# Expert layer of a two-layer backbone block: the way back from expert slots to token rows once per pair of experts

## The chip, the cores and the metric

One core of a Trainium2 chip runs the whole program. The metric is the device time of one execution in microseconds (us). The engines are TensorE (PE in the profile; PEld is its loading of the stationary operand), VectorE (DVE), ScalarE (ACT), GpSimd (POOL) and SyncE (SP, whose queue issues the weight transfers).

## The reference, cut to what matters

The program computes two layers of a hybrid block over 256 latent tokens and 256 context tokens, model width 1024. The change lies in the second layer's expert network, which works on the 256 latent tokens only:

```python
logits = jnp.dot(xf, router)
top_v, top_i = lax.top_k(logits, 2)
top_w = jax.nn.softmax(top_v, axis=-1)
comb = einsum('tk,tke->te', top_w, one_hot(top_i, 8))
for e in range(8):
    out = out + comb[:, e:e + 1] * swiglu(xf, w_gate[e], w_up[e], w_down[e])
h = h + gt2 * out          # gt2: one gate value per column, the same for all rows
return rms_norm(h, final_norm)
```

`swiglu` is `(silu(x @ w_gate) * (x @ w_up)) @ w_down` with an inner width of 1408. All numbers are float32.

## The kernel before, in words

**Matrix products.** A float32 product is made of three products of a faster type (`fp32r`): each operand is split into a high part and a remainder. For a weight tile, `load` (lines 889 to 896) takes a raw tile `wraw` that a transfer of the SP queue has brought (`fetch`, L886), ScalarE rounds it to `whi` (L893), and VectorE subtracts, `wlo = wraw - whi` (L895). `mm3` (L917 to L919) then issues three matmuls: high by high, high by remainder, remainder by high. In the expert layer there are 7 buffers of `wraw` and 4 each of `whi` and `wlo`; a raw tile is 512 KB (384 KB in the third column chunk).

**Routing.** `moe_route` gives each token a slot in each of its two experts. `moe_pass` with base 0 handles the first 128 slots of every expert; a second pass (base 128) stands in a conditional block and runs only if some expert has more than 128 tokens. Experts are taken in pairs: `gather(g)` (L1603 to L1617) collects the token columns of experts 2g and 2g+1 by matmuls with 0/1 matrices, and `back(...)` (L1619 to L1633) transposes the 0/1 matrices into `oT` (tile `ohT`), one 256-column slice for each expert `ee` of the pair, and makes the slot weights `wsl`. The order of calls is: expert 2g, gather of pair g+1, expert 2g+1.

**One expert** (`expert`, from L1646). Three column chunks of the inner width (512, 512, 384): four weight loads each for gate and up, the results in PSUM banks `mm`, then silu (L1665, ScalarE), product (L1666, VectorE), transposes (L1670) into PSUM banks `aa`, and the split into the inner rows `hFh` and `hFl` (L710, L711). Then 11 loads of the down weight, accumulated over the inner width in the PSUM banks `oo0` and `oo1` (128 slots by 1024 columns).

**The way back.** `scaled` multiplies each half by the slot weight and splits it into `yxh` (ScalarE, L1684) and `yxl` (VectorE, L1685). `finish` then calls `back(nh, i, eng)` four times, for two token tiles `i` and two column halves `nh`. Each call spreads the 128 slots over 128 token rows with two matmuls into one `aa` bank (L1693), multiplies by the gate `g2b` on VectorE into `yt` (L1695), and adds to the token rows `H` (L1696). The add is done by GpSimd; of the last expert's four, three are done by VectorE. `finish` is put on a list and called within the next expert, at its third pair of loads (`AFT = (0, 2)`, L1655); the last expert's is called at once (L1707). So there are eight ways back: seven inside experts 1 to 7, one behind expert 7.

Each tile name has a number of buffers (`s.bufs`, L1718): two for `hFh`, `hFl`, `yxh`, `yxl`, four for `yt`. The PSUM banks of `aa` are 1, 2, 3 and 5, taken in turn. The order of the instructions on each engine is not exactly that of the source: a scheduler of the framework places them by readiness and source order, so that parts of a way back or of a gather can stand between the matmuls of a load.

Of the kernel before, what the change touches and what calls it, by code (L numbers as in the profile page):

```python
# [847 lines left out]
class Full(Kern):  # L848
# [747 lines left out]
    def moe_pass(s, pool, ax, xT_h, xT_l, pos, weights, base):  # L1596
        nc = s.nc
        if base:
            p2 = s.tile(pool, [128, 2, 8], "pos2")
            nc.vector.tensor_scalar(p2, pos, -float(base), None, ALU.add)  # L1600
            pos = p2

        def gather(g):  # L1603

            es = slice(g * 2, g * 2 + 2)
            oh = s.tile(pool, [128, 2, 2, 128], "oh", F32R)
            nc.vector.tensor_tensor(oh, bc(bc(ax["iota"], 2, 1), 2, 1), bc(pos[:, :, es], 128, 3), ALU.is_equal)
            ohf = oh.bitcast(F32)
            xg = [s.tile(pool, [128, 8, 2, 128], t, F32R) for t in ("xgh", "xgl")]
            for k in range(8):  # L1610
                ps = s.tile(s.ps, [128, 512], "aa")
                for j, src in enumerate((xT_h, xT_l)):
                    for i in range(2):
                        nc.tensor.matmul(ps[:, j * 256:j * 256 + 256], src[:, i, k * 128:k * 128 + 128], oh[:, i].rearrange("p a b -> p (a b)"), start=i == 0, stop=i == 1)
                for j in range(2):
                    nc.scalar.copy(xg[j][:, k].rearrange("p a b -> p (a b)"), ps[:, j * 256:j * 256 + 256])
            return es, ohf, xg[0], xg[1]  # L1617

        def back(es, ohf, xgh, xgl):  # L1619
            oT = s.tile(pool, [128, 2, 256], "ohT", F32R)  # L1620
            pt = s.tile(s.ps, [128, 512], "aa")
            for ee in range(2):
                for i in range(2):
                    nc.tensor.transpose(pt[:, (ee * 2 + i) * 128:(ee * 2 + i) * 128 + 128], ohf[:, i, ee], s.cst("ident"))
            nc.scalar.copy(oT.rearrange("p a b -> p (a b)"), pt)
            wsl = s.tile(pool, [128, 2], "wsl")
            pw = s.tile(s.ps, [128, 512], "aa")
            for ee in range(2):
                e = es.start + ee
                for i in range(2):  # L1630
                    nc.tensor.matmul(pw[:, ee:ee + 1], ohf[:, i, ee], s.comb[:, i, e:e + 1], start=i == 0, stop=i == 1)
            nc.vector.tensor_copy(wsl, pw[:, 0:2])
            return xgh, xgl, oT, wsl  # L1633
        G = gather(0)
        if not base:
            s.comb = weights()
        G = back(*G)
        if not base:
            s.moe_rows()
        for g in range(4):  # L1640
            s.expert(pool, g * 2, 0, *G)
            Gn = back(*gather(g + 1)) if g < 3 else None
            s.expert(pool, g * 2 + 1, 1, *G)
            G = Gn

    def expert(s, pool, e, ee, xg_h, xg_l, oT, wsl):  # L1646
        nc = s.nc
        hF_h = s.tile(pool, [128, 11, 128], "hFh", F32R)
        hF_l = s.tile(pool, [128, 11, 128], "hFl", F32R)
        for c in range(3):  # L1650
            cw = 512 if c < 2 else 384
            pg = s.tile(s.ps, [128, 512], "mm")
            pu = s.tile(s.ps, [128, 512], "mm")
            for kh in range(4):
                if (c, kh) == AFT and s.pending:  # L1655
                    s.pending.pop()()
                for nm, ps in (("g", pg), ("u", pu)):
                    hi, lo = s.load(f"x{nm}{e}{c}{kh}")
                    hi = hi.rearrange("p (k m) -> p k m", k=2)
                    lo = lo.rearrange("p (k m) -> p k m", k=2)  # L1660
                    for kk in range(2):
                        k = kh * 2 + kk
                        s.mm3(ps[:, :cw], xg_h[:, k, ee], xg_l[:, k, ee], hi[:, kk], lo[:, kk], k == 0, k == 7)
            sl = s.tile(pool, [128, 512], "xs")
            nc.scalar.activation(sl[:, :cw], pg[:, :cw], AF.Silu)  # L1665
            nc.vector.tensor_mul(sl[:, :cw], sl[:, :cw], pu[:, :cw])  # L1666
            pt = s.tile(s.ps, [128, 512], "aa")
            n = cw // 128
            for q in range(n):
                nc.tensor.transpose(pt[:, q * 128:q * 128 + 128], sl[:, q * 128:q * 128 + 128], s.cst("ident"))  # L1670
            s.split(hF_h[:, c * 4:c * 4 + n].rearrange("p a b -> p (a b)"), hF_l[:, c * 4:c * 4 + n].rearrange("p a b -> p (a b)"), pt[:, :cw])
        py = [s.tile(s.ps, [128, 512], t) for t in ("oo0", "oo1")]
        for f in range(11):
            hi, lo = s.load(f"xd{e}{f}")
            for nh in range(2):
                ns = slice(nh * 512, nh * 512 + 512)
                s.mm3(py[nh], hF_h[:, f], hF_l[:, f], hi[:, ns], lo[:, ns], f == 0, f == 10)
        wc = wsl[:, ee:ee + 1]
        parts = []

        def scaled(nh):
            yh = s.tile(pool, [128, 512], "yxh", F32R)
            yl = s.tile(pool, [128, 512], "yxl", F32R)
            nc.scalar.activation(yh, py[nh], AF.Copy, scale=wc)  # L1684
            nc.vector.scalar_tensor_tensor(yl, py[nh], wc, yh.bitcast(F32), ALU.mult, ALU.subtract)  # L1685
            parts.append((yh, yl))

        def back(nh, i, eng):
            ns = slice(nh * 512, nh * 512 + 512)
            ps = s.tile(s.ps, [128, 512], "aa")  # L1690
            o = oT[:, ee, i * 128:i * 128 + 128]
            for j in range(2):
                nc.tensor.matmul(ps, o, parts[nh][j], start=j == 0, stop=j == 1)  # L1693
            t = s.tile(pool, [128, 512], "yt")
            nc.vector.tensor_mul(t, ps, s.g2b[:, ns])  # L1695
            eng.tensor_tensor(s.h[2 + i][:, ns], s.h[2 + i][:, ns], t, ALU.add)  # L1696
        scaled(0)
        scaled(1)

        def finish():  # L1700
            for i in range(2):
                for nh in range(2):
                    back(nh, i, nc.vector if e == 7 and (nh or i) else nc.gpsimd)

        s.pending.append(finish)
        if e == 7:
            s.pending.pop()()  # L1707

# [6 lines left out]

    def moe(s, pool, out):
        nc = s.nc
        s.bufs.update(xs=2, hFh=2, hFl=2, yxh=2, yxl=2, xgh=2, xgl=2, ohT=2, oh=2, wsl=2, yt=4)  # L1718
        r = s.moe_route(pool)
        s.moe_pass(pool, *r, 0)  # L1720
        s.moe_overflow(pool, r)
# [5 lines left out]
        for i in range(2):  # L1727
            for nh in range(2):
                o = s.h[2 + i][:, hs[nh]]
                (nc.vector if i and nh else nc.gpsimd).tensor_tensor(o, o, s.fn[:, hs[nh]], ALU.mult)  # L1730
        for i in range(2):
            j = 4 + 2 * i
            rs, f = s.rsqrt1(pool, s.ss[:, j:j + 1], 1e-6 * D, f"fr{i}", s.ss[:, j + 1:j + 2])
            nc.vector.tensor_scalar(rs, rs, f, None, ALU.mult)  # L1734
            for nh in range(2):
                o = s.h[2 + i][:, hs[nh]]
# [207 lines left out]
```

## Time and profile before

| | |
|---|---|
| median of 3 runs | 2430.71 us (2422.58 to 2433.34) |
| profiled execution, its own time | 2412.98 us |
| its span, first to last instruction | 2411.2 us |
| mean granted TensorE clock | 0.970 |
| stretch of the experts with ways back inside | about 2016 to 2390 us of the span |

In the profile L12 is line 12 of the kernel; `out<-in` are tile names; a number after "idle before" or in brackets is the time that an engine stood idle in front of an instruction, and `<-` names the instruction that ended the wait. Matmuls overlap, and their ends are modelled, so that the pace of TensorE is read from the starts of its instructions. "DVE x3" in a timeline means three merged instructions.

### The profile page before, as it was taken

The numbers are of one execution on the slowest core, as the hardware profiler recorded it, in microseconds if no ns is written. First come the engines' busy times: TensorE is split into PE (matmuls) and PEld (weight loads), VectorE is DVE, ScalarE is ACT, GpSimd is POOL, SyncE is SP. The second block draws the span as 40 slices with busy tenths as digits, with TensorE's granted clock in tenths as the row PEclk, the third lists the DMA queues.
The fourth block names the chain that finished last, engine by engine and source line by source line (L and its number), as shares of the span: only waits on it lengthen the run. The fifth ranks groups of instructions, "written<-read, shape, count | busy, mean of one in ns | idle before, by whom it ended". The sixth has DMA issues, their size and how long they took to land. (4 is left out here: it accounts for less than half of the span.)

```text
span 2411.2 us, 41643 instructions
## 1 busy us (share of the span) xinstructions
PE 2262.6 (94%) x15772; PEld 1785.6 (74%) x15772; DVE 1538.5 (64%) x2994; ACT 1170.4 (49%) x2150; POOL 355.6 (15%) x307
## 2 busy tenths in 40 slices
PE   7989999999999989999998999999998989999996
PEld 4767777787667767778876777878867768878775
DVE  5776666655566453333227678777567578888897
ACT  4544444544543342222226554565363457777765
POOL 1311112101002210000013221130111211111120
PEclk9999999999999999999999999999899989999998
DMA  7343432223235424443223333322325658988895
GB/s 259 110 141 127 139 122 71 76 87 117 94 113 157 160 81 162 169 162 104 95 79 124 111 113 117 115 65 91 114 71 162 216 174 320 336 306 318 309 319 192
DMA packets 160609, 373.69 MB, mean 155 GB/s; under 512 B 18016, under 2 KB 35424, under 8 KB 160400
## 3 DMA queue, kind: packets, MB, share of 16 engines
q1 hardware_dynamic: 160400, 370.94, 45.9%
q8 instruction: 126, 2.06, 0.4%
q14 instruction: 83, 0.68, 0.1%
HBM read 345.18 MB, written 25.69 MB: 154 GB/s over the span
## 5 line engine op out<-in xcount | busy, mean ns | idle before, releaser
L895 DVE TENSOR_TENSOR wlo<-wraw,whi 128x512 fp32r<-128x512 f32 (+4 forms) x666 | 652.6, 1001 | 347.9 <-ACT whi L893 334.7
L893 ACT CAST whi<-wraw 128x512 fp32r<-128x512 f32 (+4 forms) x666 | 536.8, 820 | 557.2 <-PE mm L918 226.6
L917 PE MATMUL fl<-xh,whi 128*128 128x512 f32 (+1 forms) x816 | 317.0, 389 | 2.8 <-ACT whi L893 2.7
L919 PE MATMUL fl<-xh,wlo 128*128 128x512 f32 (+1 forms) x816 | 306.7, 376 | 6.7 <-DVE wlo L895 6.5
L918 PE MATMUL fl<-xl,whi 128*128 128x512 f32 (+1 forms) x816 | 302.4, 371 | 0.0
L919 PEld LDWEIGHTS fl<-xh,wlo 128*128 128x128 f32 x816 | 157.7, 193 | 31.6 <-DVE wlo L895 10.0
L917 PEld LDWEIGHTS fl<-xh,whi 128*128 128x128 f32 x816 | 158.0, 194 | 27.9 <-issue 6.0
L918 PEld LDWEIGHTS fl<-xl,whi 128*128 128x128 f32 x816 | 158.2, 194 | 21.3 <-issue 4.7
L917 PE MATMUL mm<-xh,whi 128*128 128x512 f32 (+1 forms) x416 | 165.6, 400 | 2.0 <-ACT pad L1797 1.0
L919 PE MATMUL mm<-xh,wlo 128*128 128x512 f32 (+1 forms) x416 | 162.5, 391 | 3.2 <-DVE wlo L895 3.1
L918 PE MATMUL mm<-xl,whi 128*128 128x512 f32 (+1 forms) x416 | 163.5, 393 | 0.0
L918 PE MATMUL mm<-wlo,xgh 128*128 128x512 f32 (+1 forms) x384 | 146.5, 381 | 15.3 <-DVE wlo L895 14.8
L917 PE MATMUL mm<-whi,xgh 128*128 128x512 f32 (+1 forms) x384 | 144.3, 378 | 0.2 <-ACT xs L1665 0.2
L919 PE MATMUL mm<-whi,xgl 128*128 128x512 f32 (+1 forms) x384 | 143.7, 374 | 0.0
L1696 POOL TENSOR_TENSOR H<-H,yt 128x512 f32<-128x512 f32 x29 | 56.1, 1960 | 392.5 <-DVE yt L1695 392.5
L918 PEld LDWEIGHTS mm<-wlo,xgh 128*128 128x128 f32 x384 | 72.2, 188 | 37.0 <-DVE wlo L895 27.0
L917 PEld LDWEIGHTS mm<-xh,whi 128*128 128x128 f32 x416 | 78.3, 189 | 27.3 <-ACT whi L893 4.9
L919 PEld LDWEIGHTS mm<-xh,wlo 128*128 128x128 f32 x416 | 78.4, 188 | 20.9 <-DVE wlo L895 4.9
L636 PEld LDWEIGHTS ch<-Pb,TT 128*128 128x128 f32 x512 | 71.8, 194 | 26.2 <-DVE Pb L630 17.3
L918 PEld LDWEIGHTS mm<-xl,whi 128*128 128x128 f32 x416 | 78.6, 189 | 16.3 <-DVE xl L711 0.8
L646 DVE SCALAR_TENSOR_TENSOR Sd<-ch,e2c,Se 64x64 f32<-64x64 f32 x192 | 53.8, 280 | 56.0 <-PE ch L641 53.4
L636 PE MATMUL ch<-Pb,TT 128*128 128x64 f32 x512 | 79.3, 278 | 8.9 <-DVE Pb L630 8.1
(527 smaller groups left out, 4688.1 us busy)
## 6 DMA issues: line engine op xcount, KB each, us to landing
wraw<-in_ws_dram SPq DMA_DIRECT2D x284, 512.0 KB
wraw<-in_ws_dram SPq DMA_DIRECT2D x302, 256.0 KB
wraw<-in_w_mod_dram SPq DMA_DIRECT2D x96, 256.0 KB
wraw<-in_ws_dram SPq DMA_DIRECT2D x64, 384.0 KB
wraw<-in_w_mod_dram SPq DMA_DIRECT2D x32, 512.0 KB
wm<-in_w_mod_dram SPq DMA_DIRECT2D x32, 256.0 KB
spg<-stg SPq DMA_DIRECT2D x24, 256.0 KB
mth<-spg SPq DMA_DIRECT2D x24, 256.0 KB
```

The lines of the kernel that those rows point to most:

```text
L636: mm(ch[:, 128 + h * 64:192 + h * 64], U.TF[:, (2 * c + h) * 64:(2 * c + h) * 64 + 128], Pb[:, hs[h]], start=True, stop=True)
L646: nc.vector.scalar_tensor_tensor(S[hr, k, hr], ch[hr, o], e2c[hr, c, :], Se[hr, hr], ALU.mult, ALU.add)
L893: s.nc.scalar.copy(hi, raw)
L895: s.follow(s.nc.vector.tensor_sub(lo, raw, hi.bitcast(F32)))
L917: mm(out, ah, bh, start=start, stop=False)
L918: mm(out, ah, bl, start=False, stop=False)
L919: mm(out, al, bh, start=False, stop=stop)
L1696: eng.tensor_tensor(s.h[2 + i][:, ns], s.h[2 + i][:, ns], t, ALU.add)
```

## The change

The two experts of a pair now share one way back. An even expert leaves its scaled parts (`yxh`, `yxl` of both halves) on `s.pair`; the odd one adds its own and puts one `finish` on the list, which is called at the same place in the following expert (or at once behind expert 7). Each call of `back` accumulates four matmuls in one `aa` bank, two for each expert, and is followed by one gate product and one add. The scaled tiles get four buffers instead of two, the inner rows one instead of two.

```diff
@@ moe_pass
+        s.pair = []
         G = gather(0)
@@ expert
         def back(nh, i, eng):
             ns = slice(nh * 512, nh * 512 + 512)
             ps = s.tile(s.ps, [128, 512], "aa")
-            o = oT[:, ee, i * 128:i * 128 + 128]
-            for j in range(2):
-                nc.tensor.matmul(ps, o, parts[nh][j], start=j == 0, stop=j == 1)
+            for q, parts in enumerate(pair):
+                for j in range(2):
+                    nc.tensor.matmul(ps, oT[:, q, i * 128:i * 128 + 128], parts[nh][j], start=q == j == 0, stop=q == j == 1)
             t = s.tile(pool, [128, 512], "yt")
             nc.vector.tensor_mul(t, ps, s.g2b[:, ns])
             eng.tensor_tensor(s.h[2 + i][:, ns], s.h[2 + i][:, ns], t, ALU.add)
         scaled(0)
         scaled(1)
+        s.pair.append(parts)
...
-        s.pending.append(finish)
+        if ee:
+            pair, s.pair = s.pair, []
+            s.pending.append(finish)
         if e == 7:
             s.pending.pop()()
@@ moe
-        s.bufs.update(xs=2, hFh=2, hFl=2, yxh=2, yxl=2, xgh=2, xgl=2, ohT=2, oh=2, wsl=2, yt=4)
+        s.bufs.update(xs=2, hFh=1, hFl=1, yxh=4, yxl=4, xgh=2, xgl=2, ohT=2, oh=2, wsl=2, yt=4)
```

## Rows read from the trace of the kernel before

**Rows 1.** Busy time by engine, 2016 to 2389.5 us: PE, PEld, DVE, ACT, POOL; clock, DMA share, GB/s
```profile
2016.00:2389.50 373.50, 357.06 (x1668) 291.61 (x1666) 331.84 (x323) 267.09 (x327) 54.84 (x28) 1.00 0.88 310
```
**Rows 2.** Waits of 2015 to 2390 us: who for whom, total us, times, longest
```profile
POOL H L1696 <- DVE yt L1695: 350.5, 10, 72.2
...
PEld mm L918 <- DVE wlo L895: 27.0, 28, 1.6
...
PE mm L918 <- DVE wlo L895: 14.8, 24, 1.1
...
ACT whi L893 <- DMA wraw<-in_ws_dram: 4.9, 17, 0.8
```
**Rows 3.** Timeline of VectorE in and after the first way back
```profile
2016.69 2.49 DVE L1695 TENSOR_TENSOR yt<-aa,SU 128x512 f32<-128x512 f32 x4 [0.90 <-PE aa L1693]
2019.09 7.60 DVE L895 TENSOR_TENSOR wlo<-wraw,whi 128x1024 fp32r<-128x1024 f32 x4
2026.61 0.67 DVE L1666 TENSOR_TENSOR xs<-xs,mm 128x512 f32<-128x512 f32 x1
```
**Rows 4.** Timeline of GpSimd: the first way back's adds
```profile
2017.46 7.01 POOL L1696 TENSOR_TENSOR H<-H,yt 128x512 f32<-128x512 f32 x4 [72.24 <-DVE yt L1695]
```
**Rows 5.** Weight remainders (L895) in 2010 to 2030 us, then in 1960 to 2010 us: ns min/median/max
```profile
L895 DVE TENSOR_TENSOR wlo<-wraw,whi x9: 1212/1225/2305, 2012.1 to 2028.3; 128x1024 fp32r<-128x1024 f32 x9
...
L895 DVE TENSOR_TENSOR wlo<-wraw,whi x34: 950/1224/1227, 1960.5 to 2005.7; 128x1024 fp32r<-128x1024 f32 x26, 128x768 fp32r<-128x768 f32 x8
```
**Rows 6.** All instructions of L1695, L1696 and L1693: count, ns min/median/max
```profile
L1695 DVE TENSOR_TENSOR yt<-aa,SU x32: 674/682/692, 2016.7 to 2394.8; 128x512 f32<-128x512 f32 x32
...
L1696 POOL TENSOR_TENSOR H<-H,yt x29: 1267/2265/2278, 2017.5 to 2392.5; 128x512 f32<-128x512 f32 x29
...
L1693 PE MATMUL aa<-yxh,ohT x32: 388/395/503, 2016.0 to 2391.0; 128*128 128x512 f32 x32
```
**Rows 7.** Timeline of weight loading (PEld): the three late remainders after the first way back
```profile
2021.15 0.19 PEld L918 LDWEIGHTS mm<-wlo,xgh 128*128 128x128 f32 x1 [0.54 <-DVE wlo L895]
...
2023.38 0.19 PEld L918 LDWEIGHTS mm<-wlo,xgh 128*128 128x128 f32 x1 [1.01 <-DVE wlo L895]
...
2025.61 0.19 PEld L918 LDWEIGHTS mm<-wlo,xgh 128*128 128x128 f32 x1 [1.01 <-DVE wlo L895]
```
**Rows 8.** Timeline of PE: undisturbed pace, then first and last matmul of that way back
```profile
2014.42 0.39 PE L919 MATMUL mm<-whi,xgl 128*128 128x512 f32 x1
...
2015.79 0.39 PE L919 MATMUL mm<-whi,xgl 128*128 128x512 f32 x1
2016.02 0.40 PE L1693 MATMUL aa<-yxh,ohT 128*128 128x512 f32 x1
...
2017.65 0.40 PE L1693 MATMUL aa<-yxl,ohT 128*128 128x512 f32 x1
2017.89 0.39 PE L917 MATMUL mm<-whi,xgh 128*128 128x512 f32 x1
```
**Rows 9.** Weight-load waits at 2010:2030, 2115:2137, 2334:2356 (experts 1, 3, 7), us, times, longest
```profile
PEld mm L918 <- DVE wlo L895: 2.6, 3, 1.0
...
PEld mm L918 <- DVE wlo L895: 5.4, 5, 1.6
...
PEld mm L918 <- DVE wlo L895: 3.9, 4, 1.2
```
**Rows 10.** The same waits at 2060:2080 and 2170:2192 (experts 2 and 4)
```profile
PEld mm L918 <- DVE wlo L895: 2.7, 3, 1.2
...
PEld mm L918 <- DVE wlo L895: 3.2, 4, 1.2
```
**Rows 11.** Timeline of the end: TensorE, then VectorE behind expert 7, then ScalarE
```profile
2389.38 0.39 PE L919 MATMUL oo<-whi,hFl 128*128 128x512 f32 x1
2390.08 1.32 PE L1693 MATMUL aa<-yxh,ohT 128*128 128x512 f32 x4 [0.31 <-ACT yxh L1684]
...
2391.74 1.89 DVE L1695 TENSOR_TENSOR yt<-aa,SU 128x512 f32<-128x512 f32 x3 [0.27 <-PE aa L1693]
...
2395.56 1.03 DVE L1696 TENSOR_TENSOR H<-H,yt 128x512 f32<-128x512 f32 x1
2399.87 0.63 ACT L1079 ACTIVATE njunk<-H 128x512 f32<-128x512 f32 x1 [5.28 <-DVEq L1751]
```
**Rows 12.** Last reads of the inner rows by expert 0, first write by expert 1
```profile
L919 PE MATMUL oo<-whi,hFl x16: 392/392/392, 1995.1 to 2005.6; 128*128 128x512 f32 x16
...
L710 ACT CAST hFh<-aa x1: 587/587/587, 2028.0 to 2028.0; 128x512 fp32r<-128x512 f32 x1
```
**Rows 13.** As Rows 1, between ways back: two of eight such stretches
```profile
1985.00:2005.00 20.00, 20.00 (x97) 17.11 (x96) 18.89 (x19) 16.85 (x19) 0.00 (x0) 1.00 0.98 376
...
2080.00:2115.00 35.00, 35.00 (x177) 30.26 (x177) 28.68 (x30) 27.18 (x39) 0.00 (x0) 1.00 0.93 334
```

## The prediction

> **What bounds the kernel now.** I read four views, in this order. First the busy time of the expert stage [rows 1]: of 373.5 us TensorE is busy for 357, VectorE for 332, and the transfers hold their engines for 0.88 of the time; the clock is at its upper level, 2.4 GHz, throughout. So TensorE sets the pace and two others stand close behind. Second the waits [rows 2]: the only large wait of TensorE is for the weight remainders `wlo` that VectorE makes. It is 27.0 us by the weight loads and 14.8 us by the matmuls, whose modelled ends hide a part. GpSimd's 350 us of waiting costs nothing; it has little to do. Third the timelines, to find where those waits lie. The seven ways back inside the stage behave alike: four gate products on VectorE, 2.49 us together, then four remainders in 7.60 us [rows 3], that is up to 2.3 us each, where one takes 1.22 us with GpSimd idle [rows 5]. Just then GpSimd adds four tiles to the token rows [rows 4]; an add, too, takes 2.27 us in the middle and 1.27 us alone [rows 6]. So VectorE loses time twice, by the products and by the adds beside its remainders. Fourth the pace of TensorE. Undisturbed, six matmuls, one weight tile, take 2015.79 - 2014.42 = 1.37 us [rows 8]. After a way back the first matmul with a remainder comes every 2.23 us, each time after 1.01 us of waiting [rows 7]. One such wait thus costs 2.23 - 1.37 = 0.86 us, 0.85 of what the row shows.
>
> In the seven windows that hold the ways back of experts 1 to 7 the row says 2.6, 2.7, 5.4, 3.2, 5.4, 3.9 and 3.9 us [rows 9, 10]; experts 5 and 6 repeat the rows of experts 3 and 7. The sum is 27.1, the whole of [rows 2]. Between ways back TensorE does not stop: 20.0 of 20 and 35.0 of 35 us [rows 13].
>
> **The change part by part.** *Matmuls.* Their number stays: eight ways back with eight become four with sixteen. A matmul of the way back takes (2017.89 - 2016.02) / 8 = 0.23 us [rows 8], like any other. TensorE gains nothing by itself.
>
> *Four ways back fall away*, those called inside experts 1, 3, 5 and 7; those inside 2, 4 and 6 and the one behind expert 7 remain. VectorE is spared 16 products of 0.68 us, 10.9 us [rows 6]. GpSimd is spared 16 adds, and with each group of four VectorE is spared three slow remainders (2.31 instead of 1.22 us [rows 5]; the mean of 7.60 / 4 in [rows 3] says the same): 12 x 1.09 = 13.1 us. Together 24.0 us of VectorE, 6.0 for each way back. What TensorE gets of that is its own wait: 2.6 + 5.4 + 5.4 + 3.9 = 17.3 us, times 0.85, 14.7 us. The bounds are 17.3 us (the rows as they stand) and 9.5 us (the share 17.3 / 27.1 of the 14.8 us in [rows 2]). I take 14.7, which comes from starts. That it is less than 24.0 fits: part of each delay is swallowed by remainders made ahead.
>
> Why both slow down is a matter of the subtraction, which reads two tiles, meeting an add which reads two. The Trainium skill, SBUF — State Buffer, section Who interferes with whom, says that a VectorE instruction with two SBUF inputs contends with a GpSimd one that reads SBUF, and that the later of the two stands still until the other is done. By that rule, with this trace's 1.27 us add, a remainder would be held for 1.27 us and the 13.1 above would be 12 x 1.27 = 15.2; the trace, with 1.09, comes near to it and decides.
>
> *Three ways back grow* to sixteen matmuls. Their waits today are 2.7 + 3.2 + 3.9 = 9.8 us by the row (experts 2 and 4, and expert 6, whose row is that of expert 7) [rows 9, 10], 8.3 at 0.85. The added 8 x 0.23 = 1.87 us of TensorE work is moved, not new, and needs no weight tile, so VectorE can catch up under it. At best it covers 1.87 each, 5.6 us together. At worst the three are like the two costly ones of today (5.4 x 0.85 = 4.6 each), 5.5 us more. The nearest row is [rows 3, 8], where the eight matmuls stand in one block: the fourth product ends at 2019.18, 1.29 us after the block (2017.89). With four matmuls to a product (0.93 us) VectorE keeps step, and its last product ends about 0.68 us after the block. I take that difference, 0.6 us each, a gain of 1.8 us.
>
> *The end.* Behind expert 7 there are eight more matmuls, 1.87 us at most. TensorE stands for 0.47 us between 2389.38 and 2390.08 (0.70 less one matmul) until ScalarE has `yxh`, and the first expert's two matmuls fit there. From then on VectorE sets the pace, from 2391.74 to 2396.59 with four products and three adds [rows 11]; TensorE needs 0.93 us per tile against 0.68 + 0.7. After it ScalarE only goes on at 2399.87. Cost 0 to 1.87 us; I take 0.5, since only the second tile can come late. The one GpSimd add and three VectorE adds there stay as they are. If the cover failed, all eight matmuls would lie open.
>
> *Buffers.* Four scaled tiles are needed, since the even expert's wait through the odd one; they are freed by the way back early in the next even expert, long before its own `scaled`. The SP queue issues weight transfers when a raw tile is free, that is after its remainder; a VectorE that is less late frees them earlier, and no transfer is moved. One buffer of inner rows means that the first split of an expert must wait for the last down matmul before it. The last read is at 2005.6, the next write at 2028.0 [rows 12]: 22 us apart, cost nothing. What covers it is that the whole of the first column chunk lies between.
>
> *Sum.* 14.7 + 1.8 - 0.5 = 16.0 us. The profiled execution took 2412.98 us by its own time (span 2411.2 and 1.8 around it), so it would take 2397.0. It lies 17.7 us under the median of the three runs; I take the same 16.0 off that median: 2430.7 - 16.0 = 2414.7 us. Half a per cent, 12.2 us, is about what a measurement of this kernel can tell from no change; the forecast lies beyond it.
>
> **The rivals.** *The transfers take over.* Between ways back they hold their engines for 0.93 to 0.98 of the time at 334 to 376 GB/s [rows 13]; over the stage it is 0.88 and 310. Faster experts want 310 x 373.5 / 357.5 = 324 GB/s on the mean, which fits, but the pauses in which the raw tiles fill up today are the very stalls that go. ScalarE already waits 4.9 us for raw tiles [rows 2], without TensorE noticing. For it speaks the 0.98; against it that TensorE is never stopped in those stretches. Should half of the gain turn into waits for `wraw`, the time is 2422.7 us, within half a per cent.
>
> *The bunched way back starves TensorE.* Place: the three that remain. If VectorE's four products stand in its queue ahead of the remainders, the remainders and, behind them, TensorE's next weight tiles wait for sixteen matmuls instead of eight. Price: each costs double the worst of today, 9.2 us, 27.6 together against 23.0 for all seven now (27.1 x 0.85), 4.6 more, and the end's whole 1.87: 2430.7 + 6.5 = 2437.2 us, slower. It decides once TensorE stops for over 7 us in one way back. Against it speaks that the longest single wait is 1.6 us [rows 2] and that the bunch spares TensorE weights while it lasts.
>
> *One buffer binds.* If an expert's split, or the transposes in front of it, waited for the expert before, TensorE would idle for up to the eleven down tiles, 11 x 1.37 = 15.1 us, at seven borders: 2536 us. It takes a scheduler that puts the next expert's first chunk before the last down matmuls; the 22 us of [rows 12] exclude it nearly wholly. The Trainium skill, Trainium Kernel Development and Optimization, section Best Practices, advises two buffers so that transfers and compute overlap; no transfer writes these tiles.
>
> *It doesn't do what it says.* If the adds on GpSimd were no cause of the slow remainders, only the products would count: 10.9 of 24.0, a gain of 7.3 us, 2423.4 us.
>
> **How the numbers follow.** Forecast 0.70 (of it 0.63 beyond half a per cent), transfers 0.14 (0.03 beyond), bunched 0.09 (half of it beyond 12.2 us slower), one buffer 0.01, adds no cause 0.06 (0.02 beyond). So faster 0.68, same 0.26, slower 0.06. The forecast's own range: gain at most 14.7 + 5.6 = 20.3, at least 9.5 - 1.87 = 7.6 with the three unchanged, so 2410.4 to 2423.1. Runs lay 8.1 below and 2.6 above the median; with 5 us below and 6 above it becomes 2405 to 2429, which takes in the transfers and the adds and leaves out the other two.
>
> **What would show it.** Right: four groups of GpSimd adds, behind expert 7 included; L1695 16 times; L1693 still 64 matmuls; 9 slow remainders instead of 21; the wait of weight loads for `wlo` near 8 us in total; expert 7 and its like without a stop. Wrong: a wait for `wraw` in front of TensorE's, a `wlo` wait of over 15 us in three places, an `hFh` split that waits for `oo` matmuls, or a stage of the same length with fewer waits.

## The result, and the profile after

| | before | after |
|---|---|---|
| median of the runs | 2420.88 us (20 runs, 2410.45 to 2433.34) | 2407.51 us (20 runs, 2400.22 to 2430.70) |
| ratio, 95% interval | | 0.9945, 0.9929 to 0.9962 |
| span of the profiled execution | 2411.2 us | 2404.7 us |
| last router matmul to end of span | 472.2 us | 459.1 us |

The change makes the kernel 0.55% faster: 2420.88 × 0.0055 = 13.3 us. The spans differ by only 6.5 us, and the first thing to learn from this case is why. The router's matmuls (L1526) stand at the end of the part in front of the experts, which the change does not touch. One row each, before and then after, of all instructions of L1526 (count, ns, first and last start):

```profile
L1526 PE MATMUL aa<-aR,hT x32: 180/256/382, 1928.0 to 1939.0; 128*128 128x8 f32 x32
```
```profile
L1526 PE MATMUL aa<-aR,hT x32: 184/256/382, 1934.8 to 1945.7; 128*128 128x8 f32 x32
```

In the execution that was profiled after, the same instructions ended 6.7 us later. Counted from there, the expert layer takes 2411.2 - 1939.0 = 472.2 us before and 2404.7 - 1945.7 = 459.1 us after: 13.2 us less before rounding, which agrees with the 13.3 of the runs. All stretches below are counted so, and are called "the stretch". The expectations of eight experiments count from a later mark, the last `xTl` subtraction on GpSimd; their figures (465.4 us before, 452.2 after) are some 7 us smaller than those here.

Waits after, 2010 to 2384 us (who for whom, total us, times, longest), answering to [rows 2]:

```profile
POOL H L1697 <- DVE yt L1696: 316.9, 3, 119.1
...
PEld mm L918 <- DVE wlo L895: 9.3, 12, 1.2
...
PE mm L918 <- DVE wlo L895: 4.7, 9, 0.8
PEld aa L1671 <- DVE xs L1667: 4.5, 9, 0.7
ACT whi L893 <- DMA wraw<-in_ws_dram: 4.1, 12, 0.8
...
PEld mm L917 <- ACT whi L893: 1.9, 3, 0.8
PEld aa L1694 <- ACT yxh L1685: 1.8, 4, 0.5
```

TensorE's wait for remainders fell from 27.0 to 9.3 us, and ScalarE's for raw tiles from 4.9 to 4.1. Busy time by engine in the same window, answering to [rows 1] (PE, PEld, DVE, ACT, POOL; clock, DMA share, GB/s):

```profile
2010.00:2384.00 374.00, 366.56 (x1744) 304.10 (x1742) 319.09 (x318) 277.51 (x352) 25.01 (x12) 1.00 0.89 320
```

TensorE is now busy for 366.6 of 374 us; the transfers went from 310 to 320 GB/s. GpSimd's timeline after shows the four places of its adds, the last a single add behind expert 7 (VectorE does the other three there):

```profile
2071.01 9.03 POOL L1697 TENSOR_TENSOR H<-H,yt 128x512 f32<-128x512 f32 x4 [119.06 <-DVE yt L1696]
2178.53 7.99 POOL L1697 TENSOR_TENSOR H<-H,yt 128x512 f32<-128x512 f32 x4 [98.49 <-DVE yt L1696]
2285.86 7.99 POOL L1697 TENSOR_TENSOR H<-H,yt 128x512 f32<-128x512 f32 x4 [99.34 <-DVE yt L1696]
2386.46 1.27 POOL L1697 TENSOR_TENSOR H<-H,yt 128x512 f32<-128x512 f32 x1 [92.62 <-DVE yt L1696]
```

**Stops by expert.** For every matmul I took the distance to the next one's start and subtracted the usual distance of that kind (0.23 us for 512 columns [rows 8]); what is left, summed from the first `yxh` of one expert to that of the next, is called the stops of that expert. It counts every cause, not only `wlo`.

| us | e1 | e2 | e3 | e4 | e5 | e6 | e7 | odd | even |
|---|---|---|---|---|---|---|---|---|---|
| before | 2.5 | 2.8 | 4.9 | 3.3 | 4.9 | 4.3 | 4.3 | 16.6 | 10.4 |
| after | 0.3 | 2.3 | 0.8 | 3.3 | 1.2 | 4.3 | 1.9 | 4.1 | 9.9 |

The gain is 12.5 us in the odd experts, whose way back has gone, and only 0.5 in the even ones, whose way back has grown. Behind the first `yxh` of expert 7 the rest took 21.9 us before and 21.4 after. 13.0 and 0.4 (before rounding) make 13.4; the stretches say 13.2.

**Why the even experts stayed as they were.** Timeline of TensorE after, the matmuls of the way back inside odd experts (three of its rows):

```profile
2124.22 0.40 PE L1694 MATMUL aa<-yxh,ohT 128*128 128x512 f32 x1
2124.45 0.40 PE L1694 MATMUL aa<-yxl,ohT 128*128 128x512 f32 x1
...
2333.34 0.50 PE L1694 MATMUL aa<-yxh,ohT 128*128 128x512 f32 x1
```

Expert 2's half of the pair is issued inside expert 3, from 2124 to 2161 us, once its scaled tiles are ready (the first at 2120); so are those of experts 4 and 6, inside 5 and 7. When `finish` comes in expert 4, only eight matmuls remain, at 2172.86 to 2179.89; before they stood at 2172.81 to 2179.85. Only in expert 2 are sixteen issued in one place (2063.71 to 2073.78, with other matmuls between them), and only there did the stops shrink, by 0.5 us. VectorE's timeline of expert 4 after, around its products:

```profile
2177.76 1.88 DVE L1696 TENSOR_TENSOR yt<-aa,SU 128x512 f32<-128x512 f32 x3
2179.56 1.35 DVE L895 TENSOR_TENSOR wlo<-wraw,whi 128x1024 fp32r<-128x1024 f32 x1
2180.84 0.68 DVE L1696 TENSOR_TENSOR yt<-aa,SU 128x512 f32<-128x512 f32 x1
2181.44 8.44 DVE L895 TENSOR_TENSOR wlo<-wraw,whi 128x1024 fp32r<-128x1024 f32 x5
```

Products and remainders mix, and five remainders in a row take 8.44 us beside GpSimd's adds: the pattern of [rows 3], unchanged in the ways back that are left. Over the stage 8 remainders take more than 1.5 us, called slow below, where 21 did before.

### The profile page after: what moved, and what is told of

Read it like the earlier page. It is cut to its first block, busy times and chain, and to the rows that moved or that the text cites. A ratio compares the mean times of both kernels' runs of the same rounds, so it can differ in the third digit from the quotient of the medians.

```text
span 2404.7 us, 41593 instructions
## 1 busy us (share of the span) xinstructions
PE 2262.7 (94%) x15772; PEld 1788.6 (74%) x15772; DVE 1514.2 (63%) x2978; ACT 1168.2 (49%) x2150; POOL 327.3 (14%) x291
## 5 line engine op out<-in xcount | busy, mean ns | idle before, releaser
L895 DVE TENSOR_TENSOR wlo<-wraw,whi 128x512 fp32r<-128x512 f32 (+4 forms) x666 | 637.1, 977 | 362.6 <-ACT whi L893 350.7
L636 PEld LDWEIGHTS ch<-Pb,TT 128*128 128x128 f32 x512 | 71.5, 193 | 26.5 <-DVE Pb L630 17.7
L1697 POOL TENSOR_TENSOR H<-H,yt 128x512 f32<-128x512 f32 x13 | 26.3, 2049 | 409.5 <-DVE yt L1696 409.5
```

The source lines that it names most:

```text
L636: mm(ch[:, 128 + h * 64:192 + h * 64], U.TF[:, (2 * c + h) * 64:(2 * c + h) * 64 + 128], Pb[:, hs[h]], start=True, stop=True)
L895: s.follow(s.nc.vector.tensor_sub(lo, raw, hi.bitcast(F32)))
```

## The experiments

Each kernel was run once or as often as is given, beside the kernel before on the same chip. Since the part in front varied by 28 us over these executions (last router matmul at 1938.0 to 1966.1), the stretch is compared. It was 459.1 and 458.7 us in two executions of the changed kernel, and 472.2 in the kernel before and again in one with the same order of instructions (one_inner_buffer); from these two pairs of executions, a thin base, I take a difference of 1 us or more for real. The part of the stretch in front of expert 0's first `yxh`, where no way back stands, took 66.3 to 67.0 us, but 65.7 in three_experts and 67.7 in lead_of_three; these two need a closer look.

| | stretch | wait for `wlo` | slow remainders | stops odd / even |
|---|---|---|---|---|
| before | 472.2 | 27.0 | 21 | 16.6 / 10.4 |
| after | 459.1 | 9.3 | 8 | 4.1 / 9.9 |
| products_only | 460.7 | 14.5 | 9 | 5.6 / 10.6 |
| adds_only | 462.7 | 15.6 | 15 | 7.8 / 10.3 |
| one_inner_buffer | 472.2 | 27.0 | 21 | 16.6 / 10.3 |
| two_places | 460.5 | 11.9 | 11 | 3.8 / 11.2 |
| spread_chunk3 | 461.4 | 9.5 | 12 | 5.3 / 11.4 |
| spread_late | 465.9 | 6.5 | 12 | 5.9 / 15.2 |
| lead_of_three | 462.4 | 13.3 | 9 | 5.6 / 11.9 |
| adds_on_vector | 459.2 | 4.7 | 0 | 3.3 / 11.0 |
| three_experts | 456.9 | 5.0 | 6 | 5.4 / 7.9 |
| sum_kept_apart | 454.5 | 2.0 | 0 | 4.3 / 2.9 |
| sum_apart_early | 454.6 | 3.6 | 0 | 5.3 / 3.0 |

The wait is the row "PEld mm <- DVE wlo" over the whole span; the down loads have a row of their own (`oo`), which is 0 to 1.0 us except in spread_late.

### Which half of a way back costs: the products or the adds

products_only is the kernel before without the adds of experts 0, 2, 4 and 6:

```diff
-            eng.tensor_tensor(s.h[2 + i][:, ns], s.h[2 + i][:, ns], t, ALU.add)
+            if e % 2:
+                eng.tensor_tensor(s.h[2 + i][:, ns], s.h[2 + i][:, ns], t, ALU.add)
```

> The kernel before, with the adds of the ways back of experts 0, 2, 4 and 6 left out (these experts do not reach the output); their matmuls and gate products stay, so that in experts 1, 3, 5 and 7 VectorE still does four products but has GpSimd idle beside it. Read: the row of weight loads waiting for wlo over the stage (27.0 us before, of it 17.3 in the four odd experts; 9.3 after the change) and the stretch from the last xTl subtraction on GpSimd to the end of the span (465.4 us before, 452.2 after). Theory (VectorE falls behind by products plus slowed remainders, and a lead of about 3 us that it has swallows the first part): the products alone are 2.7 us per way back and are nearly swallowed, so the row falls to 10 to 12 us. Rival A (every us of VectorE counts alike): 45 per cent of the odd experts' wait stays, 16 to 19 us. Rival B (the products alone matter): it stays at 24 to 27 us.

adds_only is the kernel before without the products of those experts; the adds take a scaled tile instead:

```diff
-            t = s.tile(pool, [128, 512], "yt")
-            nc.vector.tensor_mul(t, ps, s.g2b[:, ns])
+            if e % 2:
+                t = s.tile(pool, [128, 512], "yt")
+                nc.vector.tensor_mul(t, ps, s.g2b[:, ns])
+            else:
+                t = parts[nh][0].bitcast(F32)
```

> The kernel before, with the gate products of experts 0, 2, 4 and 6 left out: GpSimd adds the scaled tile itself (yxh) to the token rows, so that these experts reach the output without their gate, way back and remainder; the matmuls stay. In experts 1, 3, 5 and 7 the adds still run beside the remainders, without products. Theory (sum of both against a lead): the slowed remainders alone are 3.3 us per way back, a little over the lead of 3, so the row of weight loads waiting for wlo falls to 10 to 14 us; the adds can start earlier than before and still slow three remainders per group to 2.3 us, 21 in all. Rival A (every us alike): 18 to 20 us. Rival B (the products alone matter): 9 to 10 us, with 21 slow remainders. Rival C (the adds alone matter): 24 to 27 us.

Measured: 2410.81 and 2430.57 us, the kernel before 2420.78; adds_only came to its experts 27 us late, and its stretch is 9.5 us shorter than before. Waits for remainders, products_only and then adds_only:

```profile
PEld mm L918 <- DVE wlo L895: 14.5, 17, 1.2
```
```profile
PEld mm L918 <- DVE wlo L895: 15.6, 20, 1.2
```

What follows: leaving out the adds alone brings 11.5 of the change's 13.2 us (472.2 to 460.7), with two buffers of the scaled tiles as before, so that the four buffers of the change can be worth 1.6 us at most. Leaving out the products alone brings 9.5, though some of the adds' effect goes with them, as below. Together that is more than the change: the two causes overlap. With the products alone the odd experts stop for 5.6 us, with the adds alone for 7.8, with neither for 4.1 (the changed kernel), with both for 16.6. So the products alone cost 1.5 us; the 3.7 us of the adds (7.8 - 4.1) are no full price. The rows came out above what I had expected of either kernel, and adds_only had 15 slow remainders, not 21: its adds do not wait for products and start earlier, and in experts 1, 3, 5 and 7 they slowed 0, 1, 2 and 3 remainders, where three had been slow in each. In expert 7, the only one with three, TensorE's weight loads waited 3.6 us for `wlo` with the adds alone and 3.9 before. So the adds can stop TensorE by themselves, once they meet remainders.

An estimate from the prediction's 6.0 us of VectorE for each way back (24.0 / 4) and the 12.5 us that four of them cost, 3.1 each, would be that about 3 us per expert are free. Products alone, at 2.7 us, agree with it. Expert 7 of adds_only does not: its three slow remainders are 3.2 us longer than undisturbed ones, and expert 7 still took 52.9 us from one first `yxh` to the next, 50.7 in the changed kernel and 53.2 before. A fixed free share is not shown.

### Is the single buffer of inner rows free

The kernel before with the new buffer counts of `hFh` and `hFl` alone:

```diff
-        s.bufs.update(xs=2, hFh=2, hFl=2, yxh=2, ...
+        s.bufs.update(xs=2, hFh=1, hFl=1, yxh=2, ...
```

> The kernel before with one buffer of the inner rows hFh and hFl in place of two, nothing else changed; the order of the instructions on every engine is that of the kernel before. If the single buffer costs nothing (22 us lie between the last read and the next write), the stretch from the last router matmul to the end is 472.2 us within 0.5. If the split of an expert's first chunk has to wait, it is longer by the wait, and ScalarE's cast L710 shows a wait for the oo matmuls instead of the transposes.

Measured: 2426.65 us, the kernel before 2424.19 (17 runs, 2411.15 to 2436.16). The weight loads of remainders in this kernel (busy us, mean ns, then idle us before them and what ended it):

```profile
L918 PEld LDWEIGHTS mm<-wlo,xgh 128*128 128x128 f32 x384 | 72.3, 188 | 36.9 <-DVE wlo L895 27.0
```

What follows: the wait is 27.0 us and the stretch 472.2 us, as before. The single buffer costs nothing, so the change's difference lies in the ways back.

### Would the remaining work hurt less if it were spread

My theory after the first runs was that a way back comes as one burst against a lead of four weight tiles, so that the same work spread over an expert would fit. two_places calls half of `finish` at the third and half at the seventh pair of loads:

```diff
-AFT = (0, 2)
+AFT = ((0, 2), (1, 2))
...
-                if (c, kh) == AFT and s.pending:
-                    s.pending.pop()()
+                for _ in range(2 if (c, kh) in AFT and s.pending else 0):
+                    s.pending.pop(0)()
...
```

> The changed kernel, with the shared way back called in two halves, two of its four tiles at the third pair of loads of the first column chunk and two at the third pair of the second chunk. The work is the same. Theory (a delay of VectorE stops TensorE only as far as it exceeds a lead of about 3 us, and the lead comes back between the halves, eight loads at 1.37 against 1.13 us): each half delays by 3 us, the row of weight loads waiting for wlo falls from 9.3 to 0 to 4 us and the stretch from the last xTl subtraction to the end from 452.2 to about 446 us. Rival (the total of VectorE's work in an expert counts, wherever it stands): 8 to 10 us and 451 to 453 us.

spread_chunk3 moves the whole of it into the third chunk (`AFT = (2, 2)`):

> The changed kernel, with the shared way back called whole, but at the third pair of loads of the third column chunk (one place later by two chunks); by the framework's order its four products then stand 5, 9 and 8 instructions apart on VectorE. Theory of the burst: like the run called tile by tile, row 0 to 4 us and 443 to 447 us. Rival (the place in the source decides, a whole way back stays a burst): 8 to 10 us and 451 to 453 us.

spread_late makes the four calls of `back` one at a time, among the down loads:

```diff
-                if (c, kh) == AFT and s.pending:
-                    s.pending.pop()()
...
+            if f in (1, 3, 5, 7) and s.pending:
+                s.pending.pop(0)()
             hi, lo = s.load(f"xd{e}{f}")
...
```

> The changed kernel, with the shared way back called tile by tile at the down loads 1, 3, 5 and 7 of the following even expert, in place of all at once at the third pair of loads. The framework may issue a tile's matmuls and product earlier; in the order of VectorE's instructions the four products of a way back now stand four and more weight tiles apart. Theory (TensorE stops because products and slowed remainders come in one burst at a place where VectorE's lead is small; the two halves in the run before stood only 4 to 15 us apart, in and beside the same column chunk): each single tile delays by 0.68 + 1.1 us, which is within the lead; the row of weight loads waiting for wlo falls from 9.3 to 0 to 4 us, and the stretch from the last xTl subtraction to the end from 452.2 to 443 to 447 us. Rival (VectorE's total work in an expert counts, wherever it stands): 8 to 12 us and 451 to 454 us, as with the two halves.

lead_of_three has three buffers of `whi` and `wlo` instead of four:

> The changed kernel with three buffers of whi and wlo in place of four in the expert layer, so that VectorE and ScalarE can be one weight tile (1.37 us) less ahead of TensorE. Theory (the lead swallows the first part of each delay): each of the three shared ways back inside the stage stops TensorE some 1.4 us longer, the row of weight loads waiting for wlo rises from 9.3 to 13 to 17 us, and the stretch to the end from 452.2 to 456 to 461 us. Rival (VectorE has no lead from the buffers at these places, since it is behind already): 9 to 11 us and 452 to 454 us.

Measured: 2413.14 us for two_places (before 2420.78); 2410.03, 2423.35 and 2417.38 us for the others (before 2424.63). Their stretches are 1.4, 2.3, 6.8 and 3.3 us longer than the changed kernel's. Waits of spread_late, 2010 to 2395 us:

```profile
PEld oo L918 <- DVE wlo L895: 7.2, 10, 1.2
PEld mm L918 <- DVE wlo L895: 6.5, 11, 1.0
PEld mm L917 <- ACT whi L893: 5.9, 8, 0.8
```

and its VectorE timeline around one tile:

```profile
2098.68 0.69 DVE L1696 TENSOR_TENSOR yt<-aa,SU 128x512 f32<-128x512 f32 x1 [1.68 <-PE aa L1694]
2099.29 4.05 DVE L895 TENSOR_TENSOR wlo<-wraw,whi 128x1024 fp32r<-128x1024 f32 x3
```

What follows: spreading gained nothing anywhere, and my theory of a burst at one place falls in that form. Added to the 452.2 us from which the expectations count, their differences give 453.6, 454.5 and 459.0 us, above the rival's figures too. Two things speak in the rows. First, each single add slows a whole remainder (12 for 12 adds in spread_late), while four adds in a row slow fewer than three (8 for 12). Second, a product that is called late waits in VectorE's queue for TensorE's matmuls, 1.68 us here with remainders behind it; over the stage such waits add up to 11.3 us in spread_late, 5.7 in spread_chunk3 and 0.8 in two_places, which is the order of their stretches. The lead does count: one buffer less cost 3.3 us, a little under the least that I had expected. But not as the theory had it: 0.8 us of it lies in front of expert 0's first `yxh` and 1.4 in expert 1, which hold no way back; the three experts with ways back took 1.2 us more together, not 1.4 each. How VectorE would do with ways back spread wide and without such queue waits stays open.

### Taking the slow remainders away

adds_on_vector lets VectorE do the adds of the three ways back inside:

```diff
-                    back(nh, i, nc.vector if e == 7 and (nh or i) else nc.gpsimd)
+                    back(nh, i, nc.vector if e < 7 or nh or i else nc.gpsimd)
```

> The changed kernel, with the adds of the three shared ways back inside the stage done by VectorE in place of GpSimd. Theory (an add on GpSimd costs VectorE three slowed remainders per four adds, 3.3 us): no remainder of the three ways back is slow any more, but VectorE does 4 x 0.7 = 2.8 us of adds, so the row of weight loads waiting for wlo stays at 7 to 10 us and the stretch to the end at 451 to 453 us. Rival (an add in VectorE's own queue delays it fully, one on GpSimd is mostly free): 16 us or more and over 457 us. Rival (the standstill beside GpSimd costs more than the row shows): under 4 us and under 448 us.

Measured: 2408.98 us (before 2420.78). No remainder is slow and the wait for remainders is halved to 4.7 us, yet the stretch is the changed kernel's. VectorE's timeline in expert 6:

```profile
2287.10 1.28 DVE L1696 TENSOR_TENSOR yt<-aa,SU 128x512 f32<-128x512 f32 x2
2288.30 1.28 DVE L1697 TENSOR_TENSOR H<-H,yt 128x512 f32<-128x512 f32 x2
2289.50 1.28 DVE L1696 TENSOR_TENSOR yt<-aa,SU 128x512 f32<-128x512 f32 x2
2290.70 1.28 DVE L1697 TENSOR_TENSOR H<-H,yt 128x512 f32<-128x512 f32 x2
2291.90 4.62 DVE L895 TENSOR_TENSOR wlo<-wraw,whi 128x1024 fp32r<-128x1024 f32 x4
```

and the busy time of TensorE there (first column after the length: PE; the clock is the third from the end):

```profile
2290.00:2294.00 4.00, 0.89 (x5) 0.69 (x5) 4.00 (x6) 0.23 (x1) 0.00 (x0) 1.00 0.28 113
2294.00:2298.00 4.00, 4.00 (x12) 3.09 (x11) 3.66 (x4) 2.03 (x2) 0.00 (x0) 0.57 0.91 297
2298.00:2302.00 4.00, 4.00 (x21) 3.09 (x20) 3.05 (x4) 2.92 (x5) 0.00 (x0) 1.00 0.95 366
```

What follows: the stretch is within what was expected, the wait for remainders below it. Four products and four adds stand in one block of 4.8 us ahead of the remainders, and TensorE stops once for 3.5 us. Afterwards it runs slower: its matmuls start every 0.43 us instead of 0.23 (12 in these 4 us, 21 in the next, by the rows), and the granted clock is 0.57 on the mean, so part of the time at the lower level, 1.2 GHz. The row of waits counts the 3.5 us but not what follows them. The stops of experts 4 and 6 (4.4 and 5.5 us, before 3.3 and 4.3) hold both.

### Fewer ways back still

three_experts makes one way back for three experts (0 to 2, 3 to 5, 6 and 7), with six scaled tiles, three `ohT` and one `xs` and one `oh`:

```diff
...
-        if ee:
+        if e % 3 == 2 or e == 7:
...
```

> The changed kernel with a way back once per three experts (behind experts 2 and 5, called in 3 and 6, and the last two at the end): six scaled tiles, three tiles ohT, and one buffer each of oh and xs to make room. Two ways back lie inside the stage in place of three. Theory: 6 slow remainders in place of 8, the row of weight loads waiting for wlo at 5 to 8 us, the stretch to the end at 447 to 450.5 us, a third of what the three still cost. Rival (a way back of 24 matmuls costs more than one of 16): 9 us or more and over 451 us.

Measured: 2417.05 us (before 2424.63). The stretch is 2.2 us shorter than the changed kernel's; from the mark of the expectation it is 1.4, which gives 450.8 us, just above the theory's range. Its waits show what came in the place of `wlo` (2010 to 2395 us):

```profile
PEld aa L1671 <- DVE xs L1667: 5.6, 12, 1.2
PEld mm L918 <- DVE wlo L895: 5.0, 9, 1.2
PEld mm L917 <- ACT whi L893: 4.6, 7, 0.9
```

What follows: one way back less inside saves 4.3 us of `wlo` (9.3 to 5.0), and 3.8 us of it come back as waits for `whi` and `xs` (4.6 + 5.6 against 1.9 + 4.5). So the 2.2 us are mostly not the way back's. From the first `yxh` of expert 0 to that of expert 7 this kernel took 369.8 us, the changed one 370.7, only 0.9 more, and the stops differ by 0.7. The other 1.2 us lie in front, where it took 65.7 us at a mean granted clock of 0.90 and the changed kernel 66.9 at 0.88. The single `xs` has a part in the waits, so this kernel doesn't tell the number of ways back alone.

### A version that keeps both causes off the remainders

sum_kept_apart sums the ways back before the gate: ScalarE copies the first from PSUM, VectorE adds those called in experts 4 and 6 straight from PSUM, and for these sums gate and token rows come once, behind the last remainder of expert 7; the last way back, behind expert 7, stays as it was. The four tiles `acc` take the room of two buffers of `yt`. No GpSimd add then stands beside a remainder inside the stage.

```diff
             t = s.tile(pool, [128, 512], "yt")
+            a = s.acc[i * 2 + nh]
+            if e == 1:
+                nc.scalar.copy(a, ps)
+                return
+            if e < 7:
+                nc.vector.tensor_tensor(a, ps, a, ALU.add)
+                return
...
+        if e == 7:
...
+                    m = nc.vector.tensor_mul(a, a, s.g2b[:, ns])
...
+                    nc.gpsimd.tensor_tensor(s.h[2 + i][:, ns], s.h[2 + i][:, ns], a, ALU.add)
...
```

> The changed kernel, with the sum of the experts kept in four tiles of its own before the gate: the way back in expert 2 is copied from PSUM by ScalarE, those in experts 4 and 6 are added by VectorE straight from PSUM (one instruction in place of product and add), and behind expert 7's last remainder VectorE multiplies the four tiles by the gate and GpSimd adds them to the token rows, while TensorE ends its down matmuls. GpSimd does nothing beside the remainders. Stretch from the last router matmul (L1526) to the end of the span: 472.2 us before, 459.1 after the change. Theory (VectorE has some 3 us to spare per expert; what goes over stops TensorE): expert 2 is spared all 6 us, experts 4 and 6 have 2.7 us in place of 6, so the row of weight loads waiting for wlo falls from 9.3 to 0 to 4 us with no slow remainder; the stretch falls to 451 to 455 us, less 0 to 1 us given back at the end; timed, 0.7 to 1.0 per cent faster than the kernel before. Rival (some other engine takes the place at once: ScalarE's whi, or the products' place): row under 4 us but the stretch at 457 us or more, and a ratio like that of the change, 0.9945.

The changed kernel ran beside it:

> The changed kernel once more, timed on the same chip as the run beside it. Expected: the stretch from the last router matmul to the end at 459 us within 0.5, however long the part in front of it takes in this execution; ratio 0.993 to 0.997. If the theory were wrong that the 6.5 us by which the first two profiled spans differ is 13 us gained in the expert stage less 7 us of chance in front of it, the part in front would again be longer than the kernel before's by 7 us in the same run.

sum_apart_early multiplies by the gate early in expert 7, so that only the adds stand at its end:

```diff
+                if e == 7 and (c, kh) == (0, 2):
+                    for j, a in enumerate(s.acc):
...
+                        m = nc.vector.tensor_mul(a, a, s.g2b[:, ns])
...
```

> As the run in which the sum of the experts is kept apart, which gave back 2.8 us behind expert 7 (VectorE's four gate products and GpSimd's four adds slowed each other to 4.68 and 6.29 us and stood ahead of the last way back). Here the four products stand early in expert 7, after its first two pairs of loads and with GpSimd idle, and GpSimd's four adds wait for the last remainder. Theory (2.4 us of products fit into what VectorE has to spare in an expert; four adds alone take 5.1 us, done before the last way back needs the rows): expert 7 loses 0 to 1 us, the end gets back 1.5 to 2.8 us, the stretch from the last router matmul to the end falls from 454.5 to 451.5 to 453.5 us; timed against the kernel before 0.990 to 0.994. Rival (the products in one burst stop TensorE in expert 7 as a whole way back did, about 3 us): 454 us or more.

Measured in 9 to 12 runs each: sum_kept_apart 2399.62 us, 0.9931 of the kernel before (0.9903 to 0.9959); the changed kernel beside it 2406.78 us, 0.9955 (0.9931 to 0.9979); sum_apart_early 2406.64 us against 2424.19, 0.992 (0.9893 to 0.9948). The ends of sum_kept_apart and sum_apart_early:

```profile
2365.28 4.68 DVE L1712 TENSOR_TENSOR acc<-acc,SU 128x512 f32<-128x512 f32 x4
2366.04 6.29 POOL L1714 TENSOR_TENSOR H<-H,acc 128x512 f32<-128x512 f32 x4 [421.81 <-DVE acc L1712]
```
```profile
2390.91 5.01 POOL L1716 TENSOR_TENSOR H<-H,acc 128x512 f32<-128x512 f32 x4 [422.33 <-DVE wlo L895]
```

What follows: no slow remainder is left, the wait for `wlo` falls to 2.0 us and the stops of experts 1 to 7 from 14.0 to 7.2. Of these 6.8 us the end takes back 2.8 (24.3 us behind the first `yxh` of expert 7 against 21.4), where products and adds slow each other. Moving the products forward saves 1.0 us there and costs as much in expert 7, so that the stretch came out with the rival's, though the products stopped TensorE for 1 us and not 3. By the stretch both are 4 to 4.6 us ahead of the change; by the runs they are the fastest, but the intervals overlap with the change's, so that their lead rests on the stretches. The waits that are left in sum_kept_apart are mostly for `xs` (3.4 us), `yxh` (2.9) and `whi` (1.9).

The changed kernel's second execution has the stretch as expected (458.7 us), but its front part was long again: the router's last matmul at 1945.4 us, as at 1945.7 before, against 1939.0. That by itself would fit a change that lengthens the front part. Two things speak against it: one_inner_buffer, whose instructions in front are those of the kernel before in number and order on VectorE, ScalarE and GpSimd, came there at 1952.7 us, and the medians differ by 11.6 and 13.3 us, not by 6.5.

## Why the prediction was right

The direction, the place and the mechanism held, and 2407.51 us lies inside the range. As a difference, 16.0 us were forecast and 13.3 measured; the median of the kernel before was itself 9.8 us lower in 20 runs than in the three shown, which is why the forecast of 2414.7 lies above the result although its gain was too large. In this the time was lucky: the forecast's own bounds, 2410.4 to 2423.1, miss 2407.51, and it lies inside the stated range by the 5 us that were added for the scatter of the runs.

- **Four ways back fall away, 14.7 us.** Measured 12.5 us of stops in the odd experts. The wait for `wlo` went as priced: the odd windows' 17.3 us of [rows 9] shrank to 0.4 us. What the term left out is what is late next: in the same experts TensorE now waits 2.0 us for `whi`, for which it did not wait before; its waits for `xs` there are 2.7 us as before. The rate of 0.85 held if every wait is counted: all weight-load waits fell from 32.8 us (27.0 for `wlo`, 4.0 for `xs`, 1.5 for `yxh`, 0.3 in the down loads) to 17.5, and 15.3 × 0.85 = 13.0 is what the stops lost. One reading of the term was loose: 7.60 us for four remainders [rows 3] are 2.7 us more than four times 1.22, not three times 1.09; in the trace the slow remainders of the four odd experts are 12.5 us longer than undisturbed ones, where 13.1 was reckoned.
- **VectorE loses time twice.** Right: products_only removes one cause, adds_only the other and half of the first, each is faster by more than 9 us, and 8 slow remainders were left where 9 were forecast. The rival that the adds are no cause would leave products_only at a gain near nothing; it gained 11.5 us. But the two are not additive, as the 24.0 us and the rival's share of it have them.
- **Three ways back grow, a gain of 1.8 us.** This step failed. It took sixteen matmuls to stand together in experts 2, 4 and 6 and give VectorE time. They do so in expert 2 alone; the scheduler issues the even expert's eight inside the odd one, and the way back in experts 4 and 6 is the old one (eight matmuls, the first and last start 7.04 us apart in expert 4 before and 7.03 after). Measured 0.5. The other bound, ways back as dear as the worst, came no nearer, for the same reason.
- **The end, a cost of 0.5 us.** Measured a gain of 0.1 to 0.4: behind the first `yxh` of expert 7 the changed kernel took 21.4 us, the kernel before 21.9, and one_inner_buffer, which does the same there, 21.6. Again only eight matmuls stand there, since expert 6's were issued inside expert 7. Its rows after, answering to [rows 11], TensorE, then VectorE, then ScalarE:

```profile
2383.33 0.40 PE L919 MATMUL oo<-whi,hFl 128*128 128x512 f32 x1
2384.04 1.31 PE L1694 MATMUL aa<-yxh,ohT 128*128 128x512 f32 x4 [0.31 <-ACT yxh L1685]
...
2385.69 1.89 DVE L1696 TENSOR_TENSOR yt<-aa,SU 128x512 f32<-128x512 f32 x3 [0.26 <-PE aa L1694]
...
2393.62 0.63 ACT L1079 ACTIVATE njunk<-H 128x512 f32<-128x512 f32 x1 [5.09 <-DVEq L1755]
```

  From the last down matmul to ScalarE's going on it is 10.3 us; before it was 10.5.
- **One buffer of inner rows, nothing.** Right: one_inner_buffer has the stretch and the wait of the kernel before.
- **The rivals.** The transfers did not take over: 320 GB/s, close to the 324 worked out, and ScalarE waits less for raw tiles than before. The bunch did not starve TensorE, the longest wait for a remainder is 1.2 us; but it hardly came to the test, since sixteen matmuls came in one place in expert 2 alone, spread over 10 us. adds_on_vector shows what that rival would look like, with eight VectorE instructions in one block and one stop of 3.5 us, half of the 7 us from which it was to decide.

## What to carry to other kernels

Price a removed step by the wait of the engine that sets the pace, not by the busy time it frees, and then name the wait that stood just behind it: here 17.7 us of wait for `wlo` went and 2.4 us of other waits came. Two extra loads on one engine need not cost the sum of what each is worth alone: here leaving out the adds brought 11.5 of 13.2 us, leaving out the products 9.5, so take away whichever is easier first and measure again. Where a scheduler places instructions by readiness, work that the source puts into one block need not run as one block, and a gain or a fear that rests on the block must be looked up in the timeline.

## What the runs showed of the hardware that was not expected

- **A stop can cost twice.** After TensorE's stop of 3.5 us in expert 6 of adds_on_vector its matmuls started every 0.43 us instead of 0.23 and the granted clock was 0.57 from 2294 to 2298 us; from 2298 on it was 1.00 again. It does not take so long a stop: in expert 4 of the same run the longest stretches without a matmul's start are 1.17 us (from 2181.19) and 1.02 us (from 2182.82), and the clock fell there too. Rows as above:

```profile
2182.00:2186.00 4.00, 2.77 (x12) 2.07 (x13) 4.00 (x6) 1.29 (x4) 0.00 (x0) 0.87 0.27 92
2186.00:2190.00 4.00, 4.00 (x14) 3.24 (x13) 3.28 (x3) 1.93 (x2) 0.00 (x0) 0.70 0.91 313
2190.00:2194.00 4.00, 4.00 (x22) 3.28 (x21) 3.51 (x4) 3.62 (x6) 0.00 (x0) 1.00 0.99 370
```

  The stops of up to 1.6 us in the kernel before [rows 2, 7] left the clock at 1.00 [rows 1]. What sets the two cases apart stays open here.
- **Which operands meet counts.** The product that reads one tile from PSUM takes 0.67 to 0.69 us also beside GpSimd's adds [rows 6]. The product in sum_kept_apart that reads two SBUF tiles takes 4.68 / 4 = 1.17 us beside them, and GpSimd's adds take 6.29 us instead of 5.01; with GpSimd idle, in sum_apart_early, the same product takes 0.68 us:

```profile
L1663 DVE TENSOR_TENSOR acc<-acc,SU x4: 683/684/684, 2347.6 to 2349.4; 128x512 f32<-128x512 f32 x4
```

  The Trainium skill, SBUF — State Buffer, section Who interferes with whom, says that a VectorE instruction with at most one SBUF input, outside its two-port modes, does not contend with GpSimd, and one with two does; these rows agree.
- **The part in front varies.** With the part in front of the experts unchanged, the router's last matmul started anywhere from 1938.0 to 1966.1 us. For a difference of half a per cent inside one stage, the stage's own stretch is the better measure of a single execution.
